# Retention/HGRN2 step on eight cores: early x loads untied, own buffers for the first four x tiles, g_post spread by matmul, and new DMA constants in the static scheduler

## Chip, cores and metric

The program runs on the 8 cores of one Trainium2 chip (cores 0 to 3 are one die, 4 to 7 the other). The time is the device time of the slowest core, in microseconds (us). Most executions agree within a per cent; some fall in a slower state, in which one die shows a lower granted TensorE clock (one run of the kernel before took 544.1 us, with 0.79 to 0.81 on cores 0 to 3 and 0.93 to 0.94 on the others), and those are left out of every ratio below. A profile shows one execution on its slowest core; where I compare kernels closely I use the mean over the eight cores of the profiled execution, because one core's pace differs from the next by several us.

## The reference, cut to what matters

```python
h = RMSNorm_pre(x)                      # x: 8 streams x 2048 frames x 1024, and 16 running streams x 16 frames
u = h @ W_in                            # 1024 x 4096: retention q,k,v,gate and HGRN2 q,forget,input,gate
o_r = retention(rotary(q), rotary(k), v)            # 4 heads, chunked linear recurrence with decay
o_h = hgrn2(silu(q), f = lb + (1-lb)*sigmoid(..))   # 4 heads, gated recurrence: running products of f
y = concat(silu(rg)*norm(o_r), silu(hg)*norm(o_h)) @ W_out
x <- x + RMSNorm_post(y)                # g_post is the gain of this last norm
```

Every core takes one prompt stream and two of the running streams, so all cores do the same work and share nothing but the memory.

## The kernel before

A stream is 16 tiles of 128 frames, in four blocks of four tiles. A block's x tiles are squared and summed (ScalarE), turned into a norm factor (GpSimd), scaled (VectorE), transposed (TensorE) and copied to xT; then come the projections, the rotary and HGRN chains for the q and k of eight heads, and the tile-by-tile attention with its output product. While one block is in its tile loop the next block's x tiles and heads are fed in between. The fifth to eighth x tiles are thus the second block's, and they are prepared while the first block is still being worked on.

The program does not fix the order of instructions. It lists operations with what they read and write, and a small list scheduler with its own cost model orders each engine's queue. The part of its model that the change touches, and the step that fills expected TensorE gaps in the first 30 us with dummy matmuls ("fillers", to keep the array's clock up):

```python
if name == "dma_start":
    self.cost += 800.0 if e == POOL else 400.0
    self.lat += 2000.0                               # ns from end of transfer to use
...
free_t = {e: 0.0 for e in ENGS}
...
if o["dma_key"] is not None:
    beg = max(fin, dma_free[e])
    rate = 240.0 if e == POOL else (190.0 if dma_free[POOL] > beg else 320.0)   # bytes per ns
    dma_free[e] = beg + o["nbytes"] / rate
    dlat = (dma_free[e] - fin) + o["lat"]
...
def add_fillers(self, order, filler):
    ...
            gap = ops[i]["t_start"] - prev_fin       # as the model expects it
            if gap > gap_min:
                cnt = int((gap - margin) / fdur)     # so many fillers go in
```

The loads and the first stage (cut; `[...]` marks cuts inside a line):

```python
first = [S.op(ACT, [... rows (g_pre and a decay table, 8 KB) -> rowT in QTs[1] ...]), [... lbt, glT: 4 KB each ...]]
def spread(dst, off, key, bk):            # one row to 128 partitions: ones[1x128]^T times row[1x512]
    for n in range(2):
        S.op(PE,  matmul(banks[bk[n]], lhsT=ones[0:1, :], rhs=rowT[:, off + n*512 : ...]))
        S.op(ACT, activation(dst[:, n*512:...], banks[bk[n]], Copy))
spread(gpre, 0, ...)
spread(decT[128], 1024, ...)
late_dma.append(S.op(SP, dma_start(out=gpost, in_=g_post.partition_broadcast(128))))   # 512 KB written
late_dma.append(S.op(SP, dma_start(out=decT[16], in_=dec16)))

def stage_A(xrows, L, slot, j, xbuf=None, xkey=None):       # slot = j % 2
    xid = S.op(SP, dma_start(out=xbuf, in_=xrows))
    state["nx"] += 1
    if state["nx"] in (5, 6):
        state["x_late"].append(xid)
    S.op(ACT,  activation(out=xbf[slot], in_=xbuf, func=Square, accum_out=ssx[:, slot]))  # squares overwrite xbf
    S.op(POOL, tensor_scalar(msx[:, slot], ssx[:, slot] ...)); S.op(POOL, pow -> rsx[:, slot])
    S.op(DVE,  scalar_tensor_tensor(out=xbf[slot], in0=xbuf, scalar=rsx[:, slot], in1=gpre))
    S.op(PE,   8 transposes of xbf[slot] -> Tbf)
    [... copy to xT: on DVE for the first four tiles, on ACT for later ones ...]

state["w_gate"] = w_issued[12]                # a late weight load
for xid in state["x_late"]:                   # x loads 5 and 6 wait until it has been issued
    S.ops[xid]["deps"].add(state["w_gate"])
```

x tiles 1 and 2 lie in xs[0], xs[1]; tiles 3 and 4 borrow xr[0], xr[1]; later tiles alternate in xs[0] and xs[1]. So load 7 can only start when tile 5 has been scaled out of xs[0]. Sums and scaled tiles have two places each, for four tiles.

## Time and profile before

| | before |
|---|---|
| time, median of 4 fast runs (range) | 501.7 us (500.94 to 501.77) |
| spans of the eight cores, profiled run | 494.0 to 498.7 us, mean 496.5 |
| TensorE, VectorE, GpSimd, ScalarE busy (share of span) | 84%, 60%, 55%, 42% |
| traffic of the DMA queues | 41.98 MB |
| first projection / first attention scores (mean of cores) | 26.2 / 55.3 us |
| longest TensorE pause between 65 and 100 us (mean of cores) | 12.1 us, ending at 87.3 |

How to read it: TensorE is the bound over most of the span, so a stretch before about 90 us in which it stands still can cost up to its length at the end. In the profile lines a bank is a place in PSUM where a matmul leaves its result, and an eviction is the copy out of it (to tB, tC, V, gate, xT); Wq holds the weights of the heads' q, k and forget parts, Wc those of v, input and gates; Sst is the running state. TensorE's timeline, before (start, duration, engine, line, operation, shape, count, and in brackets the idle time before it with what released it):

```profile
1.85 2.29 PE L965 MATMUL bank<-ident 128*128 128x128 bf16 x20 [1.85 <-POOL ones L473]
4.07 7.19 PE L485 MATMUL bank<-QT,ones 1*128 1x512 f32 x8
11.20 5.35 PE L965 MATMUL bank<-ident 128*128 128x128 bf16 x62
16.39 0.61 PE L545 MATMUL bank<-ident,xbf 128*128 128x128 bf16 x8
...
25.84 4.48 PE L567 MATMUL bank<-xT,Wq 128*128 128x512 bf16 x20 [0.60 <-DVE xT L550]
```

Twenty fillers, then the four row spreads (eight records, 0.90 us each), 62 more fillers until the first x tile is scaled, transposes, and at 25.84 the first projection.

### The profile page before, as it was taken

The numbers are of one execution on the slowest core, as the hardware profiler recorded it, in microseconds if no ns is written. First come the engines' busy times: TensorE is split into PE (matmuls) and PEld (weight loads), VectorE is DVE, ScalarE is ACT, GpSimd is POOL, SyncE is SP. The second block draws the span as 40 slices with busy tenths as digits, with TensorE's granted clock in tenths as the row PEclk, the third lists the DMA queues.
The fourth block names the chain that finished last, engine by engine and source line by source line (L and its number), as shares of the span: only waits on it lengthen the run. The fifth ranks groups of instructions, "written<-read, shape, count | busy, mean of one in ns | idle before, by whom it ended". The sixth has DMA issues, their size and how long they took to land.

```text
span 498.7 us, 9147 instructions; the slowest of 8 cores (494.0 to 498.7 us)
## 1 busy us (share of the span) xinstructions
PE 420.3 (84%) x2720; PEld 214.6 (43%) x2720; DVE 301.5 (60%) x628; ACT 210.6 (42%) x599; POOL 273.3 (55%) x358
## 2 busy tenths in 40 slices
PE   8897690878989799888989999999698949999754
PEld 4842240434444455444544554444344434444321
DVE  0536570755759996666599867448976485434352
ACT  4100020665234478521564863234545444555321
POOL 5688320765886666486476746664755364412210
PEclk9998896798999899999999999999989987999867
DMA  7999999223021025311102132101022202113120
GB/s 198 167 168 172 172 175 222 85 85 105 23 86 43 0 85 172 126 44 66 63 1 85 59 124 83 43 5 43 1 85 86 86 2 84 44 44 90 49 90 5
DMA packets 18290, 41.98 MB, mean 84 GB/s; under 512 B 2017, under 2 KB 7265, under 8 KB 18241
## 3 DMA queue, kind: packets, MB, share of 16 engines
q1 hardware_dynamic: 14032, 30.90, 18.9%
q0 software_dynamic: 3920, 10.49, 13.1%
q8 instruction: 22, 0.36, 0.3%
q14 instruction: 26, 0.21, 0.1%
q10 hardware_dynamic: 290, 0.02, 0.0%
HBM read 41.80 MB, written 10.09 MB: 104 GB/s over the span
## 4 chain that ended last, share of the span: by engine, by line
PE 49%; DVE 18%; issue 14%; POOL 7%; DMA 7%; ACT 4%; DVEq 0%; POOLq 0%; SPq 0%; ACTq 0%
PE bank L644 18%; PE bank L567 11%; PE bank L759 10%; DMA xs<-xp 7%; DVE tF L610 3%; DVE tE L606 3%; DVE tB L589 2%; DVE og L733 2%; POOL rsq L729 2%; PE bank L965 2%; PE bank L485 1%; PE bank L702 1%; DVE xr L776 1%; PE bank L749 1%; PE bank L704 1%
## 5 line engine op out<-in xcount | busy, mean ns | idle before, releaser
L644 PE MATMUL bank<-Wc,xT 128*128 128x512 bf16 (+1 forms) x576 | 140.0, 390 | 18.5 <-ACT tB L625 16.1
L567 PE MATMUL bank<-xT,Wq 128*128 128x512 bf16 (+1 forms) x640 | 127.1, 345 | 9.5 <-DVE tB L589 7.1
L644 PEld LDWEIGHTS bank<-Wc,xT 128*128 128x128 bf16 (+1 forms) x576 | 54.1, 99 | 82.2 <-issue 27.0
L567 PEld LDWEIGHTS bank<-xT,Wq 128*128 128x128 bf16 x640 | 53.7, 99 | 70.8 <-issue 18.4
L759 PE MATMUL bank<-Wo,ogT 128*128 128x512 bf16 (+1 forms) x288 | 74.9, 410 | 7.4 <-DVE xr L776 4.9
L733 DVE SCALAR_TENSOR_TENSOR og<-bank,rsq,gate 128x128 bf16<-128x128 f32 (+1 forms) x144 | 40.9, 342 | 14.6 <-POOL rsq L729 13.2
L587 POOL TENSOR_TENSOR tA<-qb,rotb 128x512 f32<-128x512 bf16 (+1 forms) x40 | 39.3, 986 | 17.6 <-DVE qb L581 16.4
L649 ACT ACTIVATE V<-bank 128x512 bf16<-128x512 f32 (+1 forms) x36 | 21.4, 595 | 62.5 <-PE bank L644 59.2
L759 PEld LDWEIGHTS bank<-Wo,ogT 128*128 128x128 bf16 (+1 forms) x288 | 28.0, 103 | 41.1 <-issue 17.9
L723 ACT ACTIVATE junk<-bank 128x128 bf16<-128x128 f32 (+1 forms) x144 | 37.8, 279 | 17.9 <-PE bank L704 15.5
L766 DVE TENSOR_TENSOR bank<-bank,gpost 128x512 f32<-128x512 f32 (+1 forms) x36 | 24.7, 690 | 32.3 <-ACT og L763 32.2
L729 POOL TENSOR_TENSOR rsq<-msq,mhalf 128x4 f32<-128x4 f32 (+1 forms) x36 | 40.1, 1114 | 5.2 <-POOL msq L726 0.4
L617 POOL TENSOR_TENSOR KT<-tC,tF 128x512 bf16<-128x512 f32 (+1 forms) x20 | 21.3, 1065 | 35.9 <-DVE decS L619 21.6
L538 DVE SCALAR_TENSOR_TENSOR xbf<-xs,rsx,gpre 128x1024 bf16<-128x1024 f32 (+1 forms) x16 | 24.4, 1522 | 27.0 <-POOL rsx L535 27.0
L610 DVE TENSOR_TENSOR_SCAN tF<-tC,zer 128x127 f32<-128x127 f32 (+1 forms) x72 | 38.6, 536 | 1.4 <-issue 0.2
L581 DVE TENSOR_TENSOR qb<-bank,decT 128x512 bf16<-128x512 f32 (+1 forms) x40 | 23.2, 586 | 26.6 <-PE bank L567 22.9
L606 DVE TENSOR_TENSOR_SCAN tE<-tC,zer 128x128 f32<-128x128 f32 (+1 forms) x72 | 36.4, 505 | 3.5 <-DVE tC L602 0.9
L664 POOL TENSOR_TENSOR Sst<-Sst,decS 128x1024 f32<-128x1024 f32 x15 | 28.9, 1929 | 14.8 <-DVE Sst L717 8.2
L763 ACT ACTIVATE og<-bank 128x512 bf16<-128x512 f32 (+1 forms) x36 | 21.4, 596 | 34.6 <-PE bank L759 31.0
L652 ACT ACTIVATE gate<-bank 128x512 bf16<-128x512 f32 (+1 forms) x36 | 21.4, 597 | 34.5 <-PE bank L644 33.2
L776 DVE SCALAR_TENSOR_TENSOR xr<-bank,rs,xr 128x512 f32<-128x512 f32 (+1 forms) x36 | 26.8, 746 | 12.0 <-POOL rs L773 7.8
L589 DVE TENSOR_TENSOR tB<-bank,rotb 128x512 f32<-128x512 f32 (+1 forms) x40 | 23.2, 585 | 16.2 <-PE bank L585 10.7
(86 smaller groups left out, 619.9 us busy)
## 6 DMA issues: line engine op xcount, KB each, us to landing
xr<-xp SPq DMA_DIRECT2D x18, 512.0 KB, 3.3
yp<-xr SPq DMA_DIRECT2D x16, 512.0 KB, 2.6
xs<-xp SPq DMA_DIRECT2D x14, 512.0 KB, 3.9
Wc<-w_c POOLq DMA_DIRECT2D x8, 512.0 KB, 31.2
Wq<-w_q POOLq DMA_DIRECT2D x7, 512.0 KB, 20.4
rotb<-rot_p SPq DMA_DIRECT2D x4, 512.0 KB, 10.8
Wo<-w_o POOLq DMA_DIRECT2D x4, 512.0 KB, 52.7
Wq<-w_q POOLq DMA_DIRECT2D x2, 256.0 KB, 12.1
```

Of the source, the lines that this page charges most:

```text
L567: ins = e.matmul(banks[bk][:, 0:nt], lhsT=Wq[:, pc, kc, :], rhs=xT[:, kc, 0:nt], start=(kc == 0), stop=(kc == 7))
L587: S.op(POOL, lambda e: e.tensor_tensor(out=tA[ts][:, 0:nt], in0=qb[ts][:, 0:nt], in1=rotb[rslot][:, 0, 0:nt], op=ALU.mult), reads=[("qb", ...
L589: S.op(DVE, lambda e: e.tensor_tensor(out=tB[ts][:, 0:nt], in0=banks[br][:, 0:nt], in1=rotb[rslot][:, 1, 0:nt], op=ALU.mult), reads=[("ban ...
L606: S.op(DVE, lambda e, c=c: e.tensor_tensor_scan(out=tE[0][:, c * L:(c + 1) * L], data0=tC[0][:, c * L:(c + 1) * L], data1=zer[:, 0:L], ini ...
L610: S.op(DVE, lambda e, c=c: e.tensor_tensor_scan(out=tF[0][:, rsl(c * L + L - 2, L - 1)], data0=tC[0][:, rsl(c * L + L - 1, L - 1)], data1= ...
L644: ins = e.matmul(banks[bk][0:L, :], lhsT=xT[:, kc, j * L:(j + 1) * L], rhs=Wc[:, seg, kc, :], start=(kc == 0), stop=(kc == 7))
L664: S.op(POOL, lambda e: e.tensor_tensor(out=Sst[:].rearrange("p (h e) -> p h e", h=8), in0=Sst[:].rearrange("p (h e) -> p h e", h=8), in1=d ...
L723: S.op(ACT, lambda e, hq_=hq_, h=h, g=g: e.activation(out=junk[0:L, hq_ * 128:(hq_ + 1) * 128], in_=banks[BOs[g]][0:L, hq_ * 128:(hq_ + 1) ...
L729: S.op(POOL, lambda e, g=g: e.tensor_tensor(out=rsqs[os_][0:L, g * 4:(g + 1) * 4], in0=msqs[os_][0:L, g * 4:(g + 1) * 4], in1=mhalf[0:L, 0 ...
L733: S.op(DVE, lambda e, hq_=hq_, h=h, g=g: e.scalar_tensor_tensor(out=ogs[os_][0:L, h * 128:(h + 1) * 128], in0=banks[BOs[g]][0:L, hq_ * 128 ...
L759: ins = e.matmul(banks[bk][0:L, :], lhsT=ogT[:, kc, 0:L], rhs=Wo[:, n, kc, :], start=(kc == 0), stop=(kc == 7))
L776: S.op(DVE, lambda e, n=n, bk=bk: e.scalar_tensor_tensor(out=xr[slot][0:L, n * 512:(n + 1) * 512], in0=banks[bk][0:L, :], scalar=rs2[0:L, ...
```

## The change

Its intent: let the fifth and sixth x tiles come early instead of late, let the first four tiles be normalised without waiting for each other, take 512 KB off the crowded queue, and give the scheduler a model of the two kinds of DMA queue (GpSimd's for weights, SyncE's for the rest) that is nearer to what the chip does. The core of the diff:

```diff
-                        self.lat += 2000.0
+                        self.lat += 2300.0 if nbytes > 65536 or e != ACT else 6500.0
-        free_t = {e: 0.0 for e in ENGS}
+        free_t = {e: 1000.0 for e in ENGS}
-                rate = 240.0 if e == POOL else (190.0 if dma_free[POOL] > beg else 320.0)
+                rate = 300.0 if e == POOL else (320.0 if beg > dma_free[POOL] else 160.0 if beg < 14000.0 else 100.0)
+                if e == POOL and beg < 14000.0:
+                    rate = 150.0
-    rows = din("rows", [1, 2048])
-    g_post = din("g_post", [1, 1024])
+    rows = din("rows", [1, 3072])
 [... ssx, msx, rsx: 4 columns instead of 2 ...]
+        first.append(S.op(ACT, lambda e: e.dma_start(out=rowU[:, 0:1024], in_=rows[:, 2048:3072]), writes=RU, dma_key="rows2"))
+        spread(gpost, rowU, 0, ("gpost",), (BP0, BP1), RU)
-        late_dma.append(S.op(SP, lambda e: e.dma_start(out=gpost[:], in_=g_post.partition_broadcast(128)),
-                             writes=[("gpost", 0), ("gpost", 1)], dma_key="gpost"))
-            if state["nx"] in (5, 6):
-                state.setdefault("x_late", []).append(xid)
+            q = j if state["nx"] <= 4 else slot
 [... stage_A uses column q and a buffer bbuf in place of column slot and xbf[slot] ...]
-                        xid = stage_A(d["xin"](j), d["L"], j % 2, j, xbuf=xr[j % 2], xkey=("xr", j % 2))
+                        xid = stage_A(d["xin"](j), d["L"], j % 2, j, xbuf=xr[j % 2], xkey=("xr", j % 2), bbuf=ogs[j % 2],
+                                      bkey=[("og", j % 2, h) for h in range(8)])
-        for xid in state["x_late"]:
-            S.ops[xid]["deps"].add(state["w_gate"])
```

More of the change, by code (lines that the diff above doesn't have):

```diff
@@ L376, in build_nc @@
         permb = junk[:, 0:128]
-        ssx = sb("ssx", [128, 2], F32)
-        msx = sb("msx", [128, 2], F32)
-        rsx = sb("rsx", [128, 2], F32)
+        ssx = sb("ssx", [128, 4], F32)
+        msx = sb("msx", [128, 4], F32)
+        rsx = sb("rsx", [128, 4], F32)
         xTs = [sb("xT%d" % i, [128, 8, 512], BF16) for i in range(2)]
@@ L475, in build_nc @@
         rowT = QTs[1][0:1, 0:8, :].rearrange("p h l -> p (h l)").bitcast(F32)
+        rowU = KTs[1][0:1, 0:8, :].rearrange("p h l -> p (h l)").bitcast(F32)
         RK = [("QT", 1, h) for h in range(8)]
-        first = [S.op(ACT, lambda e: e.dma_start(out=rowT, in_=rows), writes=RK, dma_key="rows"),
+        RU = [("KT", 1, h) for h in range(8)]
+        first = [S.op(ACT, lambda e: e.dma_start(out=rowT, in_=rows[:, 0:2048]), writes=RK, dma_key="rows"),
                  S.op(ACT, lambda e: e.dma_start(out=lbt[:], in_=lbs.rearrange("p (r h) -> p r h", r=2)), writes=["lbt"], dma_key="lbt"),
@@ L479, in build_nc, with spread @@
                  S.op(ACT, lambda e: e.dma_start(out=glT[:], in_=gl), writes=["glT"], dma_key="glT")]
+        first.append(S.op(ACT, lambda e: e.dma_start(out=rowU[:, 0:1024], in_=rows[:, 2048:3072]), writes=RU, dma_key="rows2"))
         for k, i in enumerate(first):
             S.ops[i]["boost"] = 6e6 - 1e5 * k
-        def spread(dst, off, key, bk):
+        def spread(dst, row, off, key, bk, rk):
             for n in range(2):
-                S.op(PE, lambda e, n=n: e.matmul(banks[bk[n]][:], lhsT=ones[0:1, :], rhs=rowT[:, off + n * 512:off + (n + 1) * 512],
+                S.op(PE, lambda e, n=n: e.matmul(banks[bk[n]][:], lhsT=ones[0:1, :], rhs=row[:, off + n * 512:off + (n + 1) * 512],
@@ L486, in spread @@
                                                  start=True, stop=True),
-                     reads=["ones"] + RK, writes=[("bank", bk[n])])
+                     reads=["ones"] + rk, writes=[("bank", bk[n])])
                 S.op(ACT, lambda e, n=n: e.activation(out=dst[:, n * 512:(n + 1) * 512], in_=banks[bk[n]][:], func=AF.Copy),
                      reads=[("bank", bk[n])], writes=[key + (n,)])
-        spread(gpre, 0, ("gpre",), (BO0, BO1))
-        spread(decT[128][:].rearrange("p a h l -> p (a h l)"), 1024, ("dec", 128), (BSC, BY0))
+        spread(gpre, rowT, 0, ("gpre",), (BO0, BO1), RK)
@@ L493, in build_nc @@
+        spread(decT[128][:].rearrange("p a h l -> p (a h l)"), rowT, 1024, ("dec", 128), (BSC, BY0), RK)
+        spread(gpost, rowU, 0, ("gpost",), (BP0, BP1), RU)
         late_dma = []
-        late_dma.append(S.op(SP, lambda e: e.dma_start(out=gpost[:], in_=g_post.partition_broadcast(128)),
-                             writes=[("gpost", 0), ("gpost", 1)], dma_key="gpost"))
         late_dma.append(S.op(SP, lambda e: e.dma_start(out=decT[16][:], in_=dec16), writes=[("dec", 16, 0), ("dec", 16, 1)], dma_key="dec16"))
@@ L516, in set_ret_dec, with stage_A @@
                      reads=["glT"], writes=[("decS", bp, c, h) for h in range(4)])
-        def stage_A(xrows, L, slot, j, xbuf=None, xkey=None):
+        def stage_A(xrows, L, slot, j, xbuf=None, xkey=None, bbuf=None, bkey=None):
             bp = state["bp"]
@@ L522, in stage_A @@
                 xbuf, xkey = xs[slot], ("xs", slot)
+            if bbuf is None:
+                bbuf, bkey = xbf[slot], [("xbf", slot)]
             xid = S.op(SP, lambda e: e.dma_start(out=xbuf[0:L, :], in_=xrows), writes=[xkey], dma_key=xkey)
             state["nx"] = state.get("nx", 0) + 1
-            if state["nx"] in (5, 6):
-                state.setdefault("x_late", []).append(xid)
             if state["nx"] <= 4:
                 S.ops[xid]["boost"] = 5e6 - 2e5 * (state["nx"] - 1) if state["nx"] == 1 else 4.4e6 - 1e5 * state["nx"]
-            S.op(ACT, lambda e: e.activation(out=xbf[slot][0:L, :], in_=xbuf[0:L, :], func=AF.Square,
-                                             accum_out=ssx[0:L, slot:slot + 1]),
-                 reads=[xkey], writes=[("ssx", slot), ("xbf", slot)])
@@ L532, in stage_A @@
-            S.op(POOL, lambda e: e.tensor_scalar(out=msx[0:L, slot:slot + 1], in0=ssx[0:L, slot:slot + 1],
+            q = j if state["nx"] <= 4 else slot
+            S.op(ACT, lambda e: e.activation(out=bbuf[0:L, :], in_=xbuf[0:L, :], func=AF.Square,
+                                             accum_out=ssx[0:L, q:q + 1]),
+                 reads=[xkey], writes=[("ssx", q)] + bkey)
+            S.op(POOL, lambda e: e.tensor_scalar(out=msx[0:L, q:q + 1], in0=ssx[0:L, q:q + 1],
                                                 scalar1=1.0 / D_MODEL, scalar2=EPS, op0=ALU.mult, op1=ALU.add),
-                 reads=[("ssx", slot)], writes=[("msx", slot)])
@@ L535, in stage_A @@
-            S.op(POOL, lambda e: e.tensor_tensor(out=rsx[0:L, slot:slot + 1], in0=msx[0:L, slot:slot + 1],
+                 reads=[("ssx", q)], writes=[("msx", q)])
+            S.op(POOL, lambda e: e.tensor_tensor(out=rsx[0:L, q:q + 1], in0=msx[0:L, q:q + 1],
                                                  in1=mhalf[0:L, 0:1], op=ALU.pow),
-                 reads=[("msx", slot), "mhalf"], writes=[("rsx", slot)])
-            S.op(DVE, lambda e: e.scalar_tensor_tensor(out=xbf[slot][0:L, :], in0=xbuf[0:L, :], scalar=rsx[0:L, slot:slot + 1],
+                 reads=[("msx", q), "mhalf"], writes=[("rsx", q)])
@@ L539, in stage_A @@
+            S.op(DVE, lambda e: e.scalar_tensor_tensor(out=bbuf[0:L, :], in0=xbuf[0:L, :], scalar=rsx[0:L, q:q + 1],
                                                        in1=gpre[0:L, :], op0=ALU.mult, op1=ALU.mult),
-                 reads=[xkey, ("rsx", slot), ("gpre", 0), ("gpre", 1)], writes=[("xbf", slot)])
+                 reads=[xkey, ("rsx", q), ("gpre", 0), ("gpre", 1)], writes=bkey)
             def tr(e):
@@ L544, in tr @@
                 for kc in range(8):
-                    ins = e.transpose(out=Tbf[:, kc * L:(kc + 1) * L], in_=xbf[slot][0:L, kc * 128:(kc + 1) * 128],
+                    ins = e.transpose(out=Tbf[:, kc * L:(kc + 1) * L], in_=bbuf[0:L, kc * 128:(kc + 1) * 128],
                                       identity=ident[0:L, 0:L])
                 return ins
-            S.op(PE, tr, reads=[("xbf", slot), "ident"], writes=["bT"])
+            S.op(PE, tr, reads=bkey + ["ident"], writes=["bT"])
             if state["nx"] <= 4:
@@ L1014 @@
     w_o = np.ascontiguousarray(w_out[0].reshape(8, 128, 2, 512).transpose(2, 1, 0, 3))
-    rows = np.concatenate([g_pre.reshape(1, 1024), tabs.pop("dec128")[0:1].reshape(1, 1024)], axis=1)
+    rows = np.concatenate([g_pre.reshape(1, 1024), tabs.pop("dec128")[0:1].reshape(1, 1024), g_post.reshape(1, 1024)], axis=1)
     in_maps = []
@@ L1023 @@
         m["w_q"], m["w_c"], m["w_o"], m["rows"] = w_q, w_c, w_o, rows
-        m["g_post"] = g_post
         m["lbs"] = np.ascontiguousarray(lower_bounds.reshape(2, 4, 128).transpose(2, 0, 1)).reshape(128, 8)
```

## The prediction

> **What bounds the kernel now.** I read the cores first: all eight are close (494.0 to 498.7 us, granted clock 0.936 to 0.949; core 4 is the slowest and the one shown), so there is no slow die to correct for. Then the forty slices of the page:
>
> ```profile
> PE   8897690878989799888989999999698949999754
> ACT  4100020665234478521564863234545444555321
> DMA  7999999223021025311102132101022202113120
> ```
>
> A slice is 12.5 us. TensorE is busy eight or nine tenths almost everywhere, so the long middle is a TensorE-bound pipeline; the DMA engines are full for seven slices (0 to 87 us, the weights) and then nearly idle. In that DMA-bound head is the one slice where TensorE does nothing, the seventh (a 0 after 75 us). Windows of the head, columns start:end, length, then busy time and instructions of each engine, granted clock, DMA share, GB/s:
>
> ```profile
> 0.00:26.00 26.00, 21.77 (x209) 16.47 (x210) 8.84 (x20) 8.04 (x14) 16.36 (x39) 1.00 0.92 183
> 26.00:55.00 29.00, 21.52 (x88) 8.37 (x86) 16.64 (x25) 0.60 (x1) 23.16 (x24) 0.94 1.05 170
> 55.00:75.00 20.00, 19.34 (x84) 8.39 (x84) 10.33 (x29) 4.19 (x7) 5.75 (x5) 0.91 0.97 175
> 75.00:88.60 13.60, 0.00 (x0) 0.00 (x0) 0.00 (x0) 2.44 (x5) 1.04 (x2) 0.67 0.82 201
> 88.60:100.00 11.40, 11.08 (x60) 5.47 (x60) 9.67 (x13) 7.15 (x13) 8.16 (x8) 0.79 0.29 93
> ```
>
> TensorE loses 26.0 us before its first projection (its 21.8 busy us there are fillers, row spreads and four transposes), 7.5 us in 26 to 55, and 13.6 us outright in 75 to 88.6. The timeline says why the last one is lost:
>
> ```profile
> 55.55 0.34 SPq L494 DMA_DIRECT2D gpost<-g_post  x1
> 56.04 0.54 SPq L743 DMA_DIRECT2D xr<-xp  x1
> 56.63 0.52 SPq L496 DMA_DIRECT2D decT<-dec  x1
> 57.30 1.20 SPq L523 DMA_DIRECT2D xs<-xp  x2
> 86.16 1.06 ACT L529 ACTIVATE xbf<-xs 128x1024 bf16<-128x1024 f32 x1 [15.91 <-DMA xs<-xp]
> 88.65 3.57 PE L644 MATMUL bank<-Wc,xT 128*128 128x512 bf16 x8 [14.22 <-ACT tB L625]
> ```
>
> The fifth x tile is asked for only at 57.3, because the code ties x loads 5 and 6 to a late weight load, and stands behind a rotary table, the 512 KB g_post broadcast, an xr tile and a small table on one queue that shares the DMA engines with the weights. It lands 28.7 us later, at 86.0. ScalarE meets its Square of that tile after 70.3 us and waits 15.9 us; the evictions queued behind it do not run, the projection banks fill, TensorE stops 14.2 us. The chain of waits agrees: it goes through that load. On the other cores the ScalarE wait is 10.7 to 15.7 us.
>
> **What the Trainium skill says.** "PSUM — Partial Sum Buffer", section "Engine vs sequencer instructions": "ScalarE/VectorE/GpSimdE queues are strict FIFO." The trace agrees: two ready evictions of tB run only after the Square, at 87.2. "DMA: Bandwidth & Descriptors", section "Issuing engines are not separate DMA queues": transfers of all issuers share the same 16 engines. The trace agrees: a 512 KB x tile lands in 3.4 to 3.9 us after 91 us, 28.7 in the weight phase. The same page's "Specifications" gives about 358 GB/s of HBM per core; here eight 1 MB weight pieces (f32 at the source) and 2.6 MB of other loads land between 54.9 and 87.0, 10.6 MB in 32.1 us, 330 GB/s, so the head is near that bound and any load put earlier delays weights. "TensorE: Matmul & The Clock Gate", "What's actually happening": a cold array runs at half rate and about 3.4 us of activity releases it. In the trace fillers start 0.107 us apart until about 14.4 us and 0.056 after; in between the f32 row spreads (1.71 us each) did not warm it.
>
> **The change, part by part.** Compared queue by queue, the instruction order differs only at the start: the last change on TensorE is at row 70 of 619, on ScalarE 51 of 283, on GpSimd 88 of 340, and beyond that VectorE and SyncE swap one or two. So the result is made in the first 130 us and then carried along.
>
> *1. x loads 5 and 6 free.* They now stand on SyncE directly behind the first rotary table and wait only for the first two x tiles to be read (about 17.5 and 18.7 us). Early x tiles land 3.0 to 4.1 us apart beside the weights and the table lands at 20.4, so I put the two at about 25 and 29. Needed: about 55. That stall is gone. Price: 1 MB at 330 GB/s, 3 us on every later weight. Weights have that slack: Wq 4-5 land at 26.1 and are wanted near 31, the first Wc half-pair at 48.5 and wanted at 55.
>
> *2. The wait moves to tiles 7 and 8.* In the new order ScalarE reaches the Square of x tile 7 after the fourth tanh, at about 76 us by the old pace. Its load is issued once tile 5 is scaled (about 57), behind rotary table, xr and the small table. Old landings on that queue: table 53.7+18.9 = 72.6, g_post 77.0, xr 81.6, small table 84.2. Without g_post and with the table asked for about 2.5 us earlier: 70, xr 74.6, small table 77.2, tile 7 at about 82, tile 8 at about 86.
>
> *3. What TensorE has done by then.* Before the wait it now also gets the last two transposes of tiles 5 and 6 (0.45 us each at the issue rate) and, in the new order, three Wc groups of 8: between the first scores and the wait the old order has 80 projection matmuls (the window counts 84 with 4 scores), the new one 104. 24 x 0.2165 us (1.73 us per 8) + 0.9 = 6.1 us ahead. It resumes when tile 7 is squared and tile 6 is evicted, 82 + 1.25 + 1.0 + 0.3 = 84.5 instead of 88.65: 4.1 us. Sum 10.2. Tile 8 holds ScalarE again about 86 to 87.3 with two groups in hand: about -1. The fourth HGRN head is scanned before the wait, not at 92 to 100 us, and TensorE lost 5.5 us in 100 to 130: about +1.
>
> *4. Own buffers for tiles 3 and 4.* Before, the third Square waited for the first transpose (17.15). Now it can run when its tile lands, 2.0+8.6 = 10.6, the fourth at 14.0. But the modelled 6.5 us for a small ScalarE load puts 95 fillers, not 20, in front of the row spreads. 95 fillers = 30 to 53 cold at 0.107 and the rest at 0.056 = 6.9 to 8.2 us, so spreads start near 9 to 10 instead of 4.1. If warm, six spreads take 6 x 0.86 = 5.1 us, if cold 10.3; then 54 fillers, 3.0 us warm. First transpose at 17.6 to 20 (the scaling cannot start before the second g_pre copy at about 15.9), against 16.5; four steps then overlap better. First projection at 25.3 to 28 against 25.84: I count 0 to -1, and up to -5 if the array goes cold.
>
> *5. g_post by matmul.* Two spreads and two 0.6 us copies in idle time, 512 KB less traffic (already counted).
>
> Sum: 10.2 - 1 + 1 - 0.5 = 9.7 us, from 501.76 to **492.0 us**.
>
> **The rivals.** *A: the wait is only renamed.* The head moves the same bytes and stays full until 87; if tile 7 lands at 86, the resume is 88.5 and only the 6.1 us ahead remain: about 496. For it: DMA share 0.97 to 1.05 until 75 us. Against it: g_post is gone from that queue. *B: the front slips.* Fillers and six spreads on an in-order TensorE put projections at 30 or later: four us of gain go, 496; with A, 500. For it: 75 more fillers on a chain that begins at 4.07. Against it: ScalarE cannot finish the fourth Square before 15.3 anyway. *C: no wait at all.* If the rotary table lands within 10 us instead of 19, tile 7 is there by 76, and the full 14 us plus about 2 come back: 486. [...]against it: both old rotary loads took 17.5 and 18.9. *D: weights late by 3 us become the bound:* a loss of 1 to 3 us in 30 to 55; against it the slack above.
>
> **Range and chances.** A or B alone leaves about 496, both about 500, C gives 486. I take 485 to 499. The 2% border is 501.76 x 0.98 = 491.7, just under my number, so faster by over 2% gets 0.47 and within 2% 0.51; slower needs a front loss of over 15 us with nothing gained: 0.02.
>
> **What would show it.** Right: the ScalarE wait for tile 5 is gone; a shorter one, about 6 us, stands at the Square of tile 7; TensorE's idle stretch shrinks from 13.6 to 4 us or less; first projection within 25 to 28; x tiles 5 and 6 land before 32; weights finish at 87 to 91; windows past 130 us are as before. Wrong: tile 7 landing at 86 (A), first projection after 30 (B), no wait for x at all (C), or projection waits for Wq in 26 to 55 (D).

## The result, and the profile after

| | before | after |
|---|---|---|
| time, median (range) of 4 fast runs each | 501.7 (500.94 to 501.77) | 490.16 (488.83 to 490.69) |
| ratio | | 0.9769, 95% interval 0.9747 to 0.9791 |
| mean span of the eight cores | 496.5 | 485.3 |
| first projection / first scores (mean of cores) | 26.2 / 55.3 | 28.3 / 54.0 |
| longest TensorE pause, 65 to 100 us: length / end | 12.1 / 87.3 | 4.4 / 83.7 |
| issue of the first y store (mean of cores) | 134.5 | 120.6 |
| DMA traffic | 41.98 MB | 41.48 MB |

A ratio here is the mean time of one kernel's fast runs over that of the other's of the same rounds, so it is not quite the ratio of the medians in the table.

The forty slices of the page, after (busy tenths; the line of the granted TensorE clock is in tenths of full speed):

```profile
PE   8997794989897997998989999999698939999734
PEclk9799898899998999999999999999798969999766
DMA  7999999421210243112011331110112202112120
```

The 0 in the seventh TensorE slice has become a 4; the seven full slices of the DMA engines are unchanged. The largest group of projections by line, before (busy us, mean ns of one; then idle us before them, and the part of it that the named releaser ended):

```profile
L644 PE MATMUL bank<-Wc,xT 128*128 128x512 bf16 (+1 forms) x576 | 140.0, 390 | 18.5 <-ACT tB L625 16.1
```

and after:

```profile
L648 PE MATMUL bank<-Wc,xT 128*128 128x512 bf16 (+1 forms) x576 | 140.1, 391 | 4.4 <-ACT tB L629 1.8
```

The matmuls cost the same; the idle time before them is 14.1 us shorter, and that behind the eviction of tB has shrunk from 16.1 to 1.8 us. What took its place is in the timeline of the kernel after (SPq lines are DMA issues on SyncE's queue; cut to loads, ScalarE's x tiles and TensorE's pause):

```profile
52.05 0.55 SPq L838 DMA_DIRECT2D rotb<-rot_p  x1
53.89 0.33 SPq L747 DMA_DIRECT2D xr<-xp  x1
54.27 0.78 SPq L499 DMA_DIRECT2D decT<-dec  x1
60.52 2.12 SPq L528 DMA_DIRECT2D xs<-xp  x2
...
82.66 1.06 ACT L533 ACTIVATE xbf<-xs 128x1024 bf16<-128x1024 f32 x1 [7.42 <-DMA xs<-xp]
...
84.86 0.59 PE L696 MATMUL bank<-ident,KT 128*128 128x128 bf16 x4 [6.02 <-ACT xT L558]
...
87.11 1.06 ACT L533 ACTIVATE xbf<-xs 128x1024 bf16<-128x1024 f32 x1 [1.42 <-DMA xs<-xp]
```

Tiles 5 and 6 no longer stop TensorE. The load of tile 7, asked for at 60.52, now does: ScalarE waits 7.42 us for it, TensorE 6.02 us behind ScalarE. On the eight cores ScalarE waits 3.3 to 7.7 us there and TensorE 1.9 to 6.3.

The windows of the kernel after (start:end, length; busy us and count of TensorE matmuls, weight loads, VectorE, ScalarE, GpSimd; granted clock, DMA share, GB/s):

```profile
26.00:55.00 29.00, 22.38 (x115) 10.27 (x116) 17.22 (x30) 2.90 (x5) 19.39 (x16) 0.99 1.06 176
55.00:75.00 20.00, 20.00 (x100) 9.27 (x99) 12.73 (x31) 6.54 (x11) 9.78 (x11) 0.94 1.01 180
75.00:88.60 13.60, 7.19 (x30) 2.87 (x28) 7.33 (x13) 4.76 (x9) 7.84 (x9) 0.75 0.94 195
88.60:100.00 11.40, 10.10 (x78) 5.55 (x76) 6.38 (x14) 8.12 (x27) 4.47 (x7) 1.00 0.30 92
100.00:110.00 10.00, 9.60 (x60) 5.01 (x61) 6.23 (x8) 7.08 (x20) 5.92 (x8) 1.00 0.32 107
110.00:120.00 10.00, 9.10 (x51) 4.28 (x50) 6.82 (x14) 1.20 (x2) 9.19 (x12) 1.00 0.16 53
120.00:130.00 10.00, 8.12 (x57) 4.31 (x56) 6.98 (x13) 3.84 (x12) 8.45 (x8) 1.00 0.28 106
```

The last three windows of the kernel before, for comparison (the earlier ones stand in the prediction):

```profile
100.00:110.00 10.00, 7.65 (x50) 4.02 (x51) 5.27 (x10) 6.67 (x24) 7.58 (x10) 1.00 0.20 58
110.00:120.00 10.00, 8.13 (x48) 4.03 (x46) 4.33 (x8) 6.52 (x11) 4.16 (x6) 0.83 0.37 113
120.00:130.00 10.00, 8.69 (x57) 4.47 (x55) 7.17 (x11) 2.92 (x12) 7.34 (x7) 1.00 0.27 95
```

Busy time alone hides one thing: a matmul at half clock is busy about twice as long (the fillers start 0.107 us apart at first and 0.056 us later). So I multiply TensorE's busy time of a window by its granted clock, which is a rough count of work in us at full speed, and take the mean over all eight cores:

| window, us | before | after | gain |
|---|---|---|---|
| 26 to 55 | 19.9 | 22.0 | +2.1 |
| 55 to 75 | 17.1 | 18.6 | +1.5 |
| 75 to 88.6 | 1.2 | 7.0 | +5.8 |
| 88.6 to 100 | 8.3 | 10.2 | +1.9 |
| 100 to 110 | 7.7 | 9.5 | +1.8 |
| 110 to 120 | 8.1 | 9.3 | +1.2 |
| 120 to 130 | 9.0 | 8.1 | -0.9 |
| sum | 71.2 | 84.6 | +13.4 |

(Of the first row's gain 1.7 us are late fillers and transposes of the kernel after, 1.1 and 0.6 us of busy time; projections alone gain little there, 83 matmuls started instead of 79. Without them the sum is 11.7.) The sum is near an independent mark, as a rough count can be: the first y store is issued 13.9 us earlier (134.5 to 120.6). The lead is still 13.6 us at the fifteenth of the sixteen prompt stores (444.3 to 430.8), 12.7 at the sixteenth (477.9 to 465.2) and 11.2 at the end of the span, so nearly all that is given back is given back behind the fifteenth.

### The profile page after: what moved, and what is told of

It reads as the page before. It is cut to its first block, busy times and chain, and to the rows that moved or that the text cites. A ratio compares the mean times of both kernels' runs of the same rounds, so it can differ in the third digit from the quotient of the medians.

```text
span 489.1 us, 9229 instructions; the slowest of 8 cores (482.2 to 489.1 us)
## 1 busy us (share of the span) xinstructions
PE 420.4 (86%) x2763; PEld 217.6 (44%) x2763; DVE 299.8 (61%) x628; ACT 210.2 (43%) x601; POOL 269.1 (55%) x358
## 2 busy tenths in 40 slices
DMA packets 18149, 41.48 MB, mean 85 GB/s; under 512 B 2002, under 2 KB 7250, under 8 KB 18099
## 4 chain that ended last, share of the span: by engine, by line
PE 49%; DVE 18%; issue 14%; POOL 7%; DMA 6%; ACT 4%; DVEq 1%; POOLq 0%; ACTq 0%; SPq 0%
PE bank L648 17%; PE bank L571 12%; PE bank L763 9%; DMA xs<-xp 6%; DVE tF L614 3%; DVE tE L610 3%; PE bank L968 3%; DVE og L737 2%; DVE tB L593 2%; POOL rsq L733 2%; PE bank L489 1%; PE bank L706 1%; POOL Sst L668 1%; PE bank L708 1%; DVE xr L780 1%
## 5 line engine op out<-in xcount | busy, mean ns | idle before, releaser
L571 PE MATMUL bank<-xT,Wq 128*128 128x512 bf16 (+1 forms) x640 | 125.7, 342 | 10.2 <-DVE tB L593 7.2
L648 PEld LDWEIGHTS bank<-Wc,xT 128*128 128x128 bf16 (+1 forms) x576 | 54.2, 99 | 68.7 <-issue 13.5
L763 PEld LDWEIGHTS bank<-Wo,ogT 128*128 128x128 bf16 (+1 forms) x288 | 27.7, 102 | 40.6 <-issue 17.1
L733 POOL TENSOR_TENSOR rsq<-msq,mhalf 128x4 f32<-128x4 f32 (+1 forms) x36 | 38.4, 1067 | 5.6 <-ACT og L767 0.4
L542 DVE SCALAR_TENSOR_TENSOR xbf<-xs,rsx,gpre 128x1024 bf16<-128x1024 f32 (+1 forms) x16 | 22.9, 1438 | 23.1 <-POOL rsx L539 19.1
L780 DVE SCALAR_TENSOR_TENSOR xr<-bank,rs,xr 128x512 f32<-128x512 f32 (+1 forms) x36 | 26.9, 746 | 12.7 <-POOL rs L777 8.9
```

Of the source, the lines that this page charges most:

```text
L571: ins = e.matmul(banks[bk][:, 0:nt], lhsT=Wq[:, pc, kc, :], rhs=xT[:, kc, 0:nt], start=(kc == 0), stop=(kc == 7))
L648: ins = e.matmul(banks[bk][0:L, :], lhsT=xT[:, kc, j * L:(j + 1) * L], rhs=Wc[:, seg, kc, :], start=(kc == 0), stop=(kc == 7))
L733: S.op(POOL, lambda e, g=g: e.tensor_tensor(out=rsqs[os_][0:L, g * 4:(g + 1) * 4], in0=msqs[os_][0:L, g * 4:(g + 1) * 4], in1=mhalf[0:L, 0 ...
L763: ins = e.matmul(banks[bk][0:L, :], lhsT=ogT[:, kc, 0:L], rhs=Wo[:, n, kc, :], start=(kc == 0), stop=(kc == 7))
L780: S.op(DVE, lambda e, n=n, bk=bk: e.scalar_tensor_tensor(out=xr[slot][0:L, n * 512:(n + 1) * 512], in0=banks[bk][0:L, :], scalar=rs2[0:L, ...
```

## The experiments

Eleven kernels ran in three batches, 3 rounds each beside the kernel before, whose medians in the batches were 502.31, 502.40 and 501.88 us. All results were correct. One table for all (means over the eight cores of the profiled run; the pause is TensorE's longest between 65 and 100 us, with its end; "store 1" is the issue of the first y store; slow runs, one each of a_gated and v_ordercut, are not in the ratios, but the medians in the table count them: the fast runs alone give 502.99 us for a_gated, 502.07 to 506.65, and 488.24 for v_ordercut):

| kernel | first projection | first scores | pause, end | store 1 | mean span | median us | ratio (95%) |
|---|---|---|---|---|---|---|---|
| before | 26.2 | 55.3 | 12.1, 87.3 | 134.5 | 496.5 | 501.7 | 1 |
| after | 28.3 | 54.0 | 4.4, 83.7 | 120.6 | 485.3 | 490.16 | 0.977 (0.975 to 0.979) |
| b_free | 26.1 | 55.2 | 8.9, 90.0 | 126.8 | 490.3 | 496.98 | 0.990 (0.987 to 0.993) |
| a_gated | 28.1 | 53.9 | 11.7, 87.7 | 134.4 | 499.2 | 503.12 | 1.003 (0.997 to 1.008) |
| a_oldmodel | 27.7 | 58.1 | 4.0, 87.6 | 124.3 | 487.1 | 491.04 | 0.977 (0.975 to 0.980) |
| a_bcast | 26.0 | 52.4 | 7.1, 87.2 | 121.6 | 485.1 | 493.04 | 0.980 (0.975 to 0.986) |
| a_twobuf | 27.9 | 56.2 | 4.4, 86.3 | 123.7 | 488.3 | 492.55 | 0.982 (0.977 to 0.987) |
| a_fewfill | 24.5 | 53.3 | 4.7, 83.5 | 120.8 | 485.7 | 491.76 | 0.980 (0.977 to 0.983) |
| a_cutfill | 26.6 | 53.2 | 4.8, 83.3 | 120.4 | 485.2 | 489.15 | 0.974 (0.971 to 0.977) |
| v_xfirst | 27.9 | 54.2 | 5.7, 89.0 | 121.5 | 486.4 | 490.38 | 0.978 (0.974 to 0.982) |
| v_xearly | 28.0 | 78.9 | 5.6, 86.6 | 120.5 | 485.8 | 489.35 | 0.976 (0.971 to 0.981) |
| v_order | 28.1 | 53.9 | 2.3, 82.9 | 117.7 | 483.9 | 489.01 | 0.975 (0.971 to 0.979) |
| v_ordercut | 26.6 | 52.8 | 2.3, 78.9 | 117.4 | 483.6 | 489.10 | 0.974 (0.969 to 0.980) |

My theory: the untied loads 5 and 6 are what the gain rests on, the wait for tile 7 is what limits it, and the front does not matter because that wait swallows it. The rivals: that the new scheduler constants or the buffers do it, that g_post's removal does it, or that something else stands right behind the wait for tile 7.

### b_free: the untied loads alone

```diff
 # kernel before
-        for xid in state["x_late"]:
-            S.ops[xid]["deps"].add(state["w_gate"])
```

> The kernel before, with only the tie of x loads 5 and 6 to the late weight load removed. Theory 1 (the freed loads carry the gain, the wait moves to x tile 7, and the g_post broadcast still stands in the queue ahead of tile 7): first projection stays near 25.8 us, no wait for tile 5, tile 7 lands at about 86 and is waited for, 494 to 498 us. Rival (the new scheduler model or the two extra buffers carry the gain): 500 us or more.

Measured: 496.98 us (496.29 to 499.5), inside the theory's range. Front and scores are as before, the wait for tile 5 is gone, and one of 8.3 to 13.5 us stands at tile 7 on ScalarE. Core 4, the slowest, timeline:

```profile
89.21 1.06 ACT L529 ACTIVATE xbf<-xs 128x1024 bf16<-128x1024 f32 x1 [11.73 <-DMA xs<-xp]
...
91.42 0.58 PE L692 MATMUL bank<-ident,KT 128*128 128x128 bf16 x4 [9.85 <-ACT xT L554]
```

So the two lines alone give a little under half of the gain (1.0 of 2.3%): TensorE has more work done before the pause (the pause begins at 90.0 - 8.9 = 81.1 us, not at 75.1), though it resumes 2.7 us later than before.

### a_gated: everything but the untied loads

```diff
 # kernel after
+            if state["nx"] in (5, 6):
+                state.setdefault("x_late", []).append(xid)
+        for xid in state["x_late"]:
+            S.ops[xid]["deps"].add(state["w_gate"])
```

> The changed kernel with x loads 5 and 6 tied to the late weight load again. Theory 1: the long wait at tile 5 returns, shorter by some 2 us because g_post is no longer ahead of it: 496 to 501 us. Rival (buffers, g_post or model carry the gain): 493 us or less.

Measured: ratio 1.0026, no gain at all, and 503 us, above the 496 to 501 I expected. Core 3, the slowest, timeline: ScalarE waits for tile 5 as in the kernel before, and TensorE, whose new order asks for that tile's transpose first, waits longer than ScalarE:

```profile
83.02 1.06 ACT L535 ACTIVATE xbf<-xs 128x1024 bf16<-128x1024 f32 x1 [11.50 <-DMA xs<-xp]
...
89.04 1.01 PE L551 MATMUL bank<-ident,xbf 128*128 128x128 bf16 x8 [13.35 <-DVE xbf L544]
```

All other parts of the change together are worth nothing while these two loads are late. The rivals that give the gain to the constants, the buffers or g_post by themselves are out.

### a_oldmodel, a_bcast, a_twobuf: one other part undone each

```diff
 # a_oldmodel: the kernel after with the three old constants of the model (and so 20 fillers in front, not 95)
-                        self.lat += 2300.0 if nbytes > 65536 or e != ACT else 6500.0
+                        self.lat += 2000.0
 [... free_t and rate likewise ...]
 # a_bcast: the kernel after with g_post as a 512 KB broadcast on SyncE again
-        first.append(S.op(ACT, [... rows2 -> rowU ...]))
-        spread(gpost, rowU, 0, ("gpost",), (BP0, BP1), RU)
+        late_dma.append(S.op(SP, lambda e: e.dma_start(out=gpost[:], in_=rows[:, 2048:3072].partition_broadcast(128)), [...]))
 # a_twobuf: the kernel after with two bf16 buffers and two columns of sums for the first four tiles
-            q = j if state["nx"] <= 4 else slot
+            q = slot
 [... and without bbuf=ogs[j % 2] ...]
```

> The changed kernel with the old constants of the scheduler (20 fillers instead of 95 before the row spreads, which then run cold). Theory 1: the front and the order of the head hardly differ, 489 to 493 us. Rival (the new model made the order that pays): 496 us or more. Second rival (the 95 fillers cost time): 487 us or less.

> The changed kernel with g_post fetched again as a 512 KB broadcast on SyncE, standing ahead of x tile 7. Theory 1: tile 7 lands 3 to 5 us later, 492 to 496 us. Rival (the head is bound by all bytes together, so one load more or less in that queue does not move tile 7's place): within 1 us of the changed kernel, 489 to 491 us.

> The changed kernel with the four first x tiles again in two bf16 buffers and two statistics columns. Theory 1 (the buffers are worth little, and the wait for tile 7 swallows a few us of the front): first projection 0 to 3 us later, 489 to 493 us. Rival (the buffers carry the gain): 496 us or more.

Measured: 491.04 us (490.09 to 492.24) with the old model: the new constants bring the first scores 4.1 us forward (58.1 to 54.0) but the time by about 1 us, within the spread; so the order of the head differs more than I expected. Of their lead, 3.7 us at the first store (124.3 to 120.6), 1.8 is left at the end; the rest goes behind the fifteenth store, as told below. 493.04 us (488.99 to 495.19) with the broadcast: its interval lies across the 2% border, "unclear". The mean span of its profiled run, 485.1, equals that of the kernel after, but that run is the fastest of its four. The traces show both sides of that exchange: with the broadcast the square of tile 7 starts 3.5 us later (mean 85.0 to 81.5), and the front is 2.3 us earlier (26.0 to 28.3), since the two spreads and their fillers are gone. 492.55 us (490.74 to 495.65) with two buffers, mean span of the profiled run 3.0 us longer; the first scores come 2.2 us later though the first projection comes 0.4 us earlier. Why the scores come later there is not settled: the order of several engines changes with the buffers.

The record has the spans of all cores for every run, so the mean over all four runs is better than that of the profiled one: 485.4 us for the kernel after, 486.3, 486.7 and 487.6 for the three, 490.9 for b_free. Undoing the three thus costs 0.9, 1.3 and 2.2 us, 4.4 together, of the 5.5 from b_free to the kernel after. Only the 2.2 of the buffers is clear of what one run differs from the next (485.0 to 486.2 against 486.5 to 488.3); that the constants and g_post carry the rest is likely, not shown.

### a_fewfill, a_cutfill: a shorter front

```diff
 # a_fewfill: the load of the rows modelled at 2.3 us, so that 25 fillers stand ahead of the spreads, not 95
-                        self.lat += 2300.0 if nbytes > 65536 or e != ACT else 6500.0
+                        self.lat += 2300.0 if nbytes > 65536 or e != ACT or n == 2048 else 6500.0
 # a_cutfill: 20 fillers instead of 54 between the spreads and the first transpose
                     cnt = int((gap - margin) / fdur)
+                    if 0 < nfill < 100:
+                        cnt = min(cnt, 20)
```

> The changed kernel with the first row load modelled at 2.3 us instead of 6.5, which puts 25 fillers before the row spreads instead of 95. Theory 1: the first projection comes 1 to 3 us earlier (25 to 27 instead of 27.8 to 28.9), but the wait for tile 7 swallows most of it, 488 to 491 us. Rival (the front is passed on in full): 486 to 488 us.

> The changed kernel with 20 instead of 54 fillers between the row spreads and the first transpose, the order otherwise the same. Theory 1 (the wait for tile 7 swallows any gain of the front): first projection near 25 instead of 27.8, 489 to 491 us. Rival (the front is passed on in full): 486.5 to 488 us.

Measured: the first projection comes 3.8 and 1.7 us earlier than in the kernel after (24.5 and 26.6 to 28.3), the first store not at all (120.8 and 120.4 to 120.6). 491.76 us (490.84 to 493.11), a little over what I expected, and 489.15 us (488.55 to 489.45). In both ScalarE still waits for tile 7, until 81.3 and 81.1 us. But that wait is not the first to swallow the faster front: the first scores come at 53.3 and 53.2 us instead of 54.0, so only 0.7 and 0.8 us are left there. TensorE waits for the last rotary product on GpSimd at that point. On core 7 of the kernel after, and on core 1 of a_fewfill, whose first projection is at 22.0:

```profile
53.42 0.38 PE L679 MATMUL bank<-QT,KT 128*128 128x128 bf16 x4 [2.64 <-POOL KT L595]
50.60 0.59 PE L679 MATMUL bank<-QT,KT 128*128 128x128 bf16 x4 [5.63 <-POOL QT L595]
```

In the mean of the cores this wait is 2.7 us in the kernel after, 5.5 in a_fewfill and 2.6 in a_cutfill. What is left at the scores is gone behind the wait for tile 7 (the pause ends at 83.5 and 83.3 instead of 83.7). So the front is indeed not passed on, but most of it is lost one wait earlier than the theory says.

### v_xfirst, v_xearly: no wait for x at all

Both start from the kernel after. v_xfirst puts the loads of tiles 7 and 8 ahead of the second rotary table, the xr tile and the small table on SyncE's queue; v_xearly has tiles 5 and 6 squared and scaled early, so that loads 7 and 8 go out long before.

```diff
 # v_xfirst
+            if state["nx"] in (7, 8):
+                S.ops[xid]["boost"] = 5e6
+        for i, o in enumerate(S.ops):
+            if [... the small table, the second rotary table, the xr tile ...]:
+                o["deps"].add(state["stt6"])          # behind the scaling of tile 6
 # v_xearly
+            if state["nx"] in (5, 6):
+                for i in (stid, stid - 1, stid - 2, stid - 3):
+                    S.ops[i]["boost"] = 3e6
+            if state["nx"] in (7, 8):
+                S.ops[xid]["boost"] = 5e6
```

> The changed kernel with one more edit: the loads of x tiles 7 and 8 stand ahead of the second rotary table, the xr tile and the small table on SyncE; the order on the compute engines is that of the changed kernel. Theory 1 (the rest of the stall is tile 7 queueing behind other loads): tile 7, issued near 60.5, lands by 77, ScalarE waits at most 2 us, the 6 us hole of TensorE at 79 to 85 closes, 484 to 487 us. Rival A (the bytes are the bound, the order is not): tile 7 lands after 81 all the same or the rotary table or a weight is waited for instead, 488 us or more.

> The changed kernel with the squares and scalings of x tiles 5 and 6 raised in priority, so that tiles 7 and 8 are asked for near 40 us, before the second rotary table. Theory 1: no wait for an x tile, 484 to 488 us, with 1 to 3 us of it given back in the rotary stage, where GpSimd and VectorE now also do the scalings. Rival A (bytes): weights come 3 us later and are waited for, 489 us or more.

Measured: 490.38 us (489.72 to 493.22) and 489.35 us (488.51 to 492.57). My theory fell: no core waits for tile 7 or 8 (ScalarE squares tile 7 at 75.2 to 76.2 us in v_xfirst), and yet nothing is won. The timeline of v_xfirst, core 6, the slowest, says what stands there instead:

```profile
75.52 0.60 ACT L607 ACTIVATE tC<-bank 128x512 f32<-128x512 f32 x1 [2.40 <-POOL KT L624]
...
83.54 1.26 POOL L624 TENSOR_TENSOR KT<-tC,tF 128x512 bf16<-128x512 f32 x1 [0.95 <-DVE tC L621]
84.76 1.26 POOL L638 TENSOR_TENSOR QT<-tB,tA 128x512 bf16<-128x512 f32 x1
...
86.45 0.55 POOL L539 TENSOR_TENSOR rsx<-msx,mhalf 128x1 f32<-128x1 f32 x1
...
87.10 1.28 DVE L542 SCALAR_TENSOR_TENSOR xbf<-xs,rsx,gpre 128x1024 bf16<-128x1024 f32 x1 [3.71 <-POOL rsx L539]
88.31 0.68 DVE L727 COPY Sst<-bank 128x512 f32<-128x512 f32 x1
...
89.14 0.59 PE L682 MATMUL bank<-QT,KT 128*128 128x128 bf16 x4 [5.79 <-DVE Sst L727]
```

The second scores of the first tile need all four HGRN heads. The fourth head's chain, from its tanh at 75.52 through VectorE's scans to its last product on GpSimd, ends at 86.0 us. Then TensorE still waits for a state copy on VectorE that the scheduler has put behind the scaling of tile 7, whose factor GpSimd delivers only after the head. In v_xearly, whose queue order puts tiles 5 and 6 ahead (hence the late first scores in the table), the pause is 5.6 us behind a mask product that stands behind the same scans on VectorE. The HGRN chain was hidden just behind the wait for tile 7. This was the last rival, and for the pause it holds; whether it also keeps the time up is the next question.

### v_order, v_ordercut: the same, with the copy ahead of the scaling

```diff
 # v_order: v_xfirst, and the scaling of tile 7 stays behind the first tile's mask product on VectorE
+        S.ops[state["stt7"]]["deps"].add(state["at1"])
 # v_ordercut: v_order, and a_cutfill's limit of 20 fillers
```

> The kernel with tiles 7 and 8 loaded first, plus one dependence that keeps the scaling of tile 7 on VectorE behind the state copy and the mask product of the first block's first tile. Theory 2 (behind the wait for tile 7 stood the chain of the fourth HGRN head on VectorE and GpSimd, and in the last run its in-order VectorE also waited for the scale of tile 7): the hole of TensorE shrinks from 5.8 to about 3 us, second scores near 86 to 87 instead of 89.1, 485 to 489 us. Rival: the time is given back further on, 489 us or more.

> Both edits together: tiles 7 and 8 first with the dependence, and 20 fillers. Theory 2: with no load waited for, the earlier front moves the HGRN chain too and is passed on, 482 to 487 us, 2 to 3 us below the run without the cut. Rival (the weights or a later load set the pace then): no faster than the run without the cut.

Measured: 489.01 us (488.38 to 491.8) and 489.10 us (487.58 to 489.96 in the fast runs). The copy no longer holds anything; on core 4 of v_order the second scores wait 2.27 us for the head itself:

```profile
86.30 0.38 PE L682 MATMUL bank<-QT,KT 128*128 128x128 bf16 x4 [2.27 <-POOL QT L638]
```

The first store is 2.9 us earlier than in the kernel after (117.7 to 120.6), but only 1.4 us of that is left at the second store, 1.5 at the sixteenth (463.7 to 465.2) and 1.4 in the mean span. So half of what the shorter pause wins is given back between the first and the second store, which is what the rival of v_order said; why was not followed. The times overlap with the kernel after. A further 1.5 us from the front (v_ordercut) moves the first store by 0.3 us. v_order is at the edge of what I expected, v_ordercut missed it. By the mean span of all fast runs they are 1.2 and 1.6 us shorter than the kernel after (484.2 and 483.8 to 485.4), but in another batch; no variant is shown to beat the changed kernel.

## Why the prediction was right or wrong

The time came out at 490.16 us for a predicted 492.0, inside the range; the gain is 2.3%, just beyond the border at which I had put nearly even chances. The mechanism was the predicted one, but that the number is so close is in part luck: behind the pause 4.0 us came that I had not counted, and behind the fifteenth store 2.4 us went that I had not counted either.

**Step 1, right.** On the core shown x tiles 5 and 6 were issued at 16.84 and 18.0 us and were squared at 27.26 and 30.21 us, predicted about 25 and 29. The stall for tile 5 is gone, and a_gated shows that restoring it takes the whole gain back. The weights did not bind between 26 and 55 us (rival D): no core of the kernel after waits for a weight there, though with the still earlier front of a_fewfill and of a_cutfill one core each waits 1.3 us for one.

**Step 2, right.** Tile 7 was squared at 82.66 us on the core shown (predicted 82) and 81.5 in the mean; tile 8 at 87.11 (predicted 86). The wait on ScalarE is 7.42 us there and 5.6 in the mean (predicted 6). g_post's absence from the queue is worth 3.5 us at tile 7 (a_bcast), so rival A is out: tile 7 did not land at 86. The reading behind it has a slip: I had swapped the two rotary loads. The first, asked for at 2.93, took 18.89 us and landed at 21.8, not 20.4; the second, asked for at 53.68, took 17.50 and landed at 71.2, not 72.6, so the old landings put 5.8 us on g_post, not 4.4. The landing came out right all the same (70.5, predicted 70) because the second table, asked for 1.6 us earlier and not 2.5, took 18.42.

**Step 3, right in the resume, mis-sized in the work done before it and after it.** Resuming at 84.5 instead of 88.65 us was predicted (4.1 us); on the core shown it was 84.86, and in the mean 83.7 instead of 87.3 (3.6). Up to 88.6 us the count gives 2.1 + 1.5 + 5.8 = 9.4 us, and 7.7 without the late fillers and transposes, against 10.2 - 0.5 predicted. And "about -1" for tile 8 and "about +1" for the fourth head, nothing together, became +4.0 us between 88.6 and 130 us (1.9 + 1.8 + 1.2 - 0.9). Busy time there rose from 35.3 to 37.2 us in the mean of the cores, and the granted clock from 0.87, 0.92 and 0.98 to 0.99, 1.00 and 1.00 in the first three windows. So 1.9 of the 4.0 us are busy time and the other 2.1 are clock: I had priced the pause by its length alone. Of the clock's 2.1 us, 1.2 lie in the window right behind the pause; 0.9 lie between 100 and 120 us, where five of the eight cores of the kernel before have another 3.4 us at half clock (on core 4 it is the 0.83 in the window from 110), which the kernel after has not. The sign "4 us or less" of TensorE's idle stretch came out at 4.4 in the mean and 6.0 on the core shown.

**Step 4, wrong in size.** The first transpose was predicted for 17.6 to 20 and began at 21.02 on the core shown; the first projection at 27.82 there and 28.3 in the mean, at and just past the late end of 25.3 to 28. The front slipped 2.1 us, where I had counted 0 to -1. The timeline after shows why:

```profile
9.38 3.69 PE L489 MATMUL bank<-QT,ones 1*128 1x512 f32 x8
12.92 3.34 PE L489 MATMUL bank<-KT,ones 1*128 1x512 f32 x4
16.20 4.99 PE L968 MATMUL bank<-ident 128*128 128x128 bf16 x54
21.02 0.61 PE L549 MATMUL bank<-ident,xbf 128*128 128x128 bf16 x8
...
27.82 3.40 PE L571 MATMUL bank<-xT,Wq 128*128 128x512 bf16 x15 [0.49 <-DVE xT L554]
```

Four spreads took 0.46 us a record, the last two 0.84, and 54 fillers 4.99 us instead of the 3.0 I gave them warm: the 95 fillers warmed the array, and it went cold again during the spreads (the granted clock on this core is 1.00 from 6.4 to 13.2 us and 0.50 from there to 20.0). I had counted either warm or cold, not a change on the way. (Two slips in the working: 53 cold and 42 warm fillers make 8.0 us, not 8.2, and on core 4 of the kernel before the fillers stand 0.107 us apart until 14.8 us, not 14.4.) But the slip of the front cost nothing: a_fewfill and a_cutfill take it out and are not shown to be faster. That this term was wrong and the time right has a reason: TensorE waits for GpSimd's rotary product at the first scores and then for tile 7, and both waits come after the front.

**Step 5, right as far as it went.** The two spreads are cheap in traffic, but not "in idle time": they stand in the front. By the traces they cost 2.3 us there and win 3.5 at tile 7; by the mean spans of all runs the exchange wins 1.3 us, which is not clear of the spread.

**What the sum left out at the other end.** I expected windows past 130 us as before. Up to the fifteenth prompt store that is nearly so: the lead is 13.9 us at the first and 13.6 at the fifteenth. Behind it 2.4 us are lost. There b_free loses 0.9 us and a_oldmodel 0.2, every kernel with the new constants 1.5 to 2.6. So most of this loss goes with the new constants. In that stretch, between the first store of a running stream and the sixteenth prompt store, the mean granted clock is 0.76 in the kernel after, 0.82 before and 0.83 in a_oldmodel; which instruction starts it stays open.

**The rivals.** A and D are out as said, B as it was put (no projection at 30). C, no wait at all, did not come about in the kernel after. v_xfirst made its condition true, and it gave 490 and not 486: rival C's arithmetic failed because it took the wait for tile 7 to be the only thing there, and the fourth HGRN head ended only at 86 us. That is not the whole of it: v_order, with a pause of 2.3 us, still took 489. I had read that chain only as something scanned "before the wait".

## What to carry to other kernels

Before pricing the removal of a wait, look for the second thing that the same engine will need at that moment: here a load (until 82 us) and a chain on two other engines (until 86 us) ended within 4 us of each other, so removing the first won nothing. A change that matters only ahead of such waits, like a faster or slower front, can be off by 2 to 4 us without moving the time; measure it at each mark behind it (first scores, end of the pause, first and last stores) and see at which it is lost. And price a TensorE pause as its length plus the time at a lower clock behind it (1.2 us here), which shows only when busy time is multiplied by the granted clock.

## What the Trainium skill lacked or had wrong

- "TensorE: Matmul & The Clock Gate", section "What's actually happening", says that activity releases the throttle and an idle window of about 3.4 us brings it back; it does not say which matmuls count as activity (elsewhere the page says so of transposes only). Here TensorE hardly stood still, yet one-row f32 matmuls (1 by 128 times 1 by 512) let the clock fall: 0.46 us a record in the first 3.7 us, 0.84 in the next 3.3, and slow fillers after them. On all eight cores of the kernel after the last four records took 2.8 to 3.8 us, and in the kernel before eight of them took 7.19 us on every core. That it was these matmuls and nothing else follows from the times alone (the granted clock of core 7 falls at 13.2 us, while they run); no run without them was made.
- The same section agrees with the long pauses: after v_xfirst's 5.7 us, ending at 89.0, the mean clock from 88.6 to 100 us is 0.77. But its idle window of about 3.4 us is not a safe limit: on four cores of the kernel after, pauses of 1.9 to 3.2 us were followed by 3.4 us at half clock (on core 6 a pause of 1.9, and 0.50 from 82.5 to 85.9), and so were the 2.3 us of v_order on three of the eight cores.
- "DMA: Bandwidth & Descriptors", section "Issuing engines are not separate DMA queues", says that all issuers share the engines; it gives no figure for how long a load takes that is issued while another queue is full. Here, under the weight loads, the 512 KB rotary table took 18.4 us and a 64 KB table behind it 23.8 us, and on ScalarE's queue two 4 KB loads took 5.7 and 9.9 us. A fixed 2 us plus size over rate, as in the old scheduler, is far off; but the new 6.5 us is too long for the 8 KB of rows, issued at 1.06 us and there by 4.07 in the kernel before, where the spreads start without a wait. That is where the 95 fillers come from.
- No page tests a count of work by windows under a changing clock. Busy time times granted clock, summed over 26 to 130 us, gave 13.4 us (11.7 without fillers and transposes of the front) where the first store moved by 13.9; for b_free 5.1 against 7.7, and for a_gated -0.3 against 0.1. It is a rough count.
